# Gathering the tokens of two experts at once, already transposed, in a mixture-of-experts encoder layer

## The chip, the cores and the metric

The kernel runs on one core of one Trainium2 chip. The metric is device time in microseconds (us) of one execution, the median of several runs. Engines are named as the profile names them: PE is the matrix engine (PEld its weight loads), DVE the vector engine, ACT the scalar engine, POOL and SP the two others; SP issues nearly all transfers. SBUF is the on-chip memory with 128 partitions, PSUM the small accumulation memory that PE writes.

## The reference, cut to what matters

One encoder layer on 256 tokens of width 1024, in float32. The front half is attention beside a gated recurrence, then an output projection and a residual add. The rest, which fills most of the time, is the expert layer:

```
logits = rms_norm(x, norm2_g) @ w_router + b_router        # 32 experts
top_v, top_i = top_k(logits, 4);  gates = softmax(top_v)
for each expert e, for the tokens xb that chose it:
    g = min(xb @ w_gate[e] + b_gate[e], 7)
    u = clip(xb @ w_up[e] + b_up[e], -7, 7)
    y = ((u + 1) * g * sigmoid(1.702 * g)) @ w_down[e] + b_down[e]
out = x + sum over the chosen experts of gate * y;   final rms_norm
```

The three weight matrices of an expert are 1024 x 1024 float32, 12 MB together; 32 experts make 384 MB, and each byte is used once.

## The kernel before, in words

Weights stream through a ring of 21 slots of 1 MB. SP issues one transfer per slot, in the order gate, up, down, four pieces each, expert after expert; a transfer waits until the piece 21 slots earlier has been used by PE.

A token that chose expert e has a position in that expert's list (`pos`). The first 64 positions are handled in the main loop. Where an expert has more, a branch (`overflow`, line 866) runs a second block of 64 on the same weights before the main one; in this run that happens ahead of experts 12 and 18.

Per expert, PE does this, in program order (lines 963 to 1019):

- `ffn1` twice (lines 828 to 837): gate and up. The expert's 64 tokens, transposed (`xT`, 64 columns per 128 features), are stationary; the weights stream, 512 columns at a time, for two halves of the output that share the array, on partitions 0 to 63 and 64 to 127. `act_gate` and `act_up` apply the nonlinearity on DVE and ACT.
- In odd experts, `pair_weights` (line 883): four transposes that turn the one-hot combine weights of two experts into `gT`.
- `gather` (line 808) for the next expert: a one-hot matrix `sl` of 64 columns, scaled by the token's norm factor, is stationary and x streams, two token tiles by two halves, 512 columns each. ACT copies the 64 x 1024 result out of PSUM.
- `h_trans` (line 850): four transposes of the hidden activations, then a copy on ACT.
- `gather_trans` (line 822): four transposes of the gathered rows, then one multiply on DVE into `xT`.
- In even experts after the first, `pair_scatter` (line 912): four matmuls of 128 x 128 x 512 that add the previous pair's outputs, weighted by the gates, to four PSUM banks (`acc`) that hold the result.
- `ffn2` (line 856): the down projection, the same shape as `ffn1`, then a copy on ACT.

Transposed slices take every second column (`column_pairs`, line 818), so that two neighbouring features sit in one partition's slice of the weights. A float32 matmul is two passes in the trace, each with a weight load of its own; a transpose is one. PSUM has two buffers (`ps`, tag pt) for gathers and transposes, used in turn.

The order on each engine is the order of the code (`manual_schedule`).

Of the kernel before, what the change touches and what calls it, by code (L numbers as in the profile page):

```python
# [10 lines left out]
F32 = mybir.dt.float32  # L11
# [4 lines left out]
OP = mybir.AluOpType  # L16
# [6 lines left out]
NT = T // 128  # L23
KC = D // 128
# [47 lines left out]
def bc(ap, shape):  # L72
    return ap.to_broadcast(shape)
# [708 lines left out]
def experts(tc, A, out, g):  # L782
    nc = tc.nc
    V, S, G, PE = nc.vector, nc.scalar, nc.gpsimd, nc.tensor
    slot, x1, pos, gates, rstd2 = g["slot"], g["x1"], g["pos"], g["gates"], g["rstd2"]
    ident, iota, emask, b3, cnti = g["ident"], g["iota"], g["emask"], g["b3"], g["cnti"]
    pcols, rsqrt, weights = g["pcols"], g["rsqrt"], g["weights"]
    with ExitStack() as ctx:
        wk = ctx.enter_context(tc.tile_pool(name="wk", bufs=1))
        ps, acc = g["psum"]["ps"], g["psum"]["acc"]  # L790
        go = wk.tile([128, 512], F32, name="go")
        Y = [wk.tile([128, 512], F32, name=f"Y{d}") for d in range(2)]
# [6 lines left out]
        def pick(dst, e, b, weight):  # L799
            for t in range(NT):  # L800
                V.tensor_scalar(dst[:, t], iota[:, b], pos[:, t, e:e + 1], weight[:, t], op0=OP.is_equal, op1=OP.mult)  # L801

        def select(e, b):
            sr = wk.tile([128, NT, 64], F32, name="sro" if b else "sr")
            pick(sr, e, b, rstd2)
            return sr

        def gather(sl):
            p = ps([128, 512])
            for t in range(NT):  # L810
                for h in range(2):
                    PE.matmul(p[h * 64:h * 64 + 64, :], lhsT=sl[:, t, :], rhs=x1[:, t, h * 512:(h + 1) * 512],  # L812
                              start=t == 0, stop=t == NT - 1)
            xr = wk.tile([128, 512], F32, name="sg", tag="sg")
            S.activation(xr, p, AF.Copy)  # L815
            return xr

        def column_pairs(a, c):

            return a[:, c // 2 * 256 + c % 2:(c // 2 + 1) * 256:2]  # L820

        def gather_trans(xr, dst):
            p = ps([128, 4, 2, 64])
            for c in range(4):
                PE.transpose(p[:, c].rearrange("p a b -> p (a b)"), column_pairs(xr, c), ident)  # L825
            V.tensor_tensor(dst.rearrange("p (h c) s -> p c h s", h=2), p, n2, OP.mult)  # L826

        def ffn1(w, xT, e, which, tag="pu"):
            p = ps([128, 512], tag, 1)
            for h in range(2):  # L830
                PE.matmul(p[h * 64:h * 64 + 64, :], lhsT=bc(emask[:, e:e + 1], [96, 64]),  # L831
                          rhs=b3[:, which, h * 512:(h + 1) * 512], start=True, stop=False)
            for k in range(KC):
                for h in range(2):
                    PE.matmul(p[h * 64:h * 64 + 64, :], lhsT=xT[:, k, :],  # L835
                              rhs=w[k // 2][:, k % 2, h * 512:(h + 1) * 512], start=False, stop=k == KC - 1)
            return p

        def act_gate(p, gp):
            sg = wk.tile([128, 512], F32, name="sg", tag="sg")  # L840
            V.tensor_scalar(gp, p, LIMIT, None, op0=OP.min)  # L841
            S.activation(sg, gp, AF.Sigmoid, scale=ALPHA)  # L842
            V.tensor_tensor(gp, gp, sg, OP.mult)  # L843

        def act_up(p, gp):
            u = wk.tile([128, 512], F32, name="sg", tag="sg")
            V.tensor_scalar(u, p, LIMIT, -LIMIT, op0=OP.min, op1=OP.max)  # L847
            V.scalar_tensor_tensor(gp, u, 1.0, gp, op0=OP.add, op1=OP.mult)  # L848
# [17 lines left out]
        def overflow(cnt, e, w, b=1):  # L866

            with tc.If(cnt > 64 * b, preferred_fallthrough_block=True, label=f"ov{e}_{b}"):  # L868
                if b < 3:
                    hint(cnt, e, b + 1)  # L870
                ov_block(e, b, *w)
                if b < 3:
                    overflow(cnt, e, w, b + 1)

        def combine(e):

            gd = wk.tile([128, NT, 2, 2, 64], F32, name="gd", tag="gd")
            for u in range(2):
                for d in range(2):
                    pick(gd[:, :, d, u ^ d, :], e - 1 + u, 0, gates[:, :, e - 1 + u:e + u])  # L880
            return gd
# [25 lines left out]
        def gate_norm():  # L907
            V.tensor_reduce(gs, gates, axis=AX.X, op=OP.add)
            V.reciprocal(gs, gs)
            V.tensor_tensor(gates, gates, bc(gs, [128, NT, E]), OP.mult)  # L910

        def pair_scatter(gT, last):
            for t in range(NT):
                for d in range(2):
                    PE.matmul(acc[t][d], lhsT=gT[:, t, d, :], rhs=Y[d], start=False, stop=last)  # L915


        def one_pick(e, b, tag):
            gdo = wk.tile([128, NT, 2, 64], F32, name=tag, tag=tag)
            for u in range(2):  # L920
                pick(gdo[:, :, u], e, b, gates[:, :, e:e + 1])
            return gdo

        def one_weights(gT, gdo):
            p = ps([128, NT, 128])
            for t in range(NT):
                PE.transpose(p[:, t, :], gdo[:, t].rearrange("p a b -> p (a b)"), ident)  # L927
            S.activation(gT, p, AF.Copy)
# [7 lines left out]
        def load_cnt(e):  # L936
            c = nc.values_load(cnti[:, e:e + 1], engines=(ET.PE, ET.DVE, ET.Activation), min_val=0, max_val=T)
            hint(c, e, 1)
            return c
# [12 lines left out]
            S.activation(go, ffn2(wd, go, 0), AF.Copy)  # L952
            one_scatter(gTo, go, False)

        sl = select(0, 0)
        xT = wk.tile([128, KC, 64], F32, name="xT")
        xr = gather(sl)
        g["open_acc"](1, 1)
        gather_trans(xr, xT)
        gate_norm()  # L960
        S.activation(ssf[:, 0, 0:1], gs[:, 0], AF.Sigmoid)
        cnt = load_cnt(0)
        for e in range(E):
            last = e == E - 1
            wg, wu, wd = weights(0, e), weights(1, e), weights(2, e)
            overflow(cnt, e, (wg, wu, wd))
            gp = wk.tile([128, 512], F32, name="gp")
            if e >= E - 2:
                gd = one_pick(e, 0, "gd")
            elif e % 2 == 1:  # L970
                gd = combine(e)
            if not last:
                sl = select(e + 1, 0)
            pg = ffn1(wg, xT, e, 0, "pg")
            if not last:
                cnt = load_cnt(e + 1)
            act_gate(pg, gp)
            if last:
                one_scatter(g0, Y[0], False, (0,))
                one_scatter(g0, Y[0], False, (1,), (0,))  # L980
                g1 = wk.tile([128, NT, 2, 128], F32, name="gT", tag="gT")[:, :, 0]
                one_weights(g1, gd)
            act_up(ffn1(wu, xT, e, 1), gp)
            if e == E - 2:
                g1 = wk.tile([128, NT, 128], F32, name="g1")
                one_weights(g1, gd)
            elif e % 2 == 1 and not last:
                gT = pair_weights(gd)
            if not last:
                xr = gather(sl)  # L990
            hT = wk.tile([128, 512], F32, name="gd", tag="gd")
            h_trans(gp, hT)
            if last:
                one_scatter(g0, Y[0], False, (1,), (1,))
            else:
                xT = wk.tile([128, KC, 64], F32, name="xT")
                gather_trans(xr, xT)
            if e % 2 == 0 and e > 0:
                pair_scatter(gT, False)
            if e == 2:  # L1000
                add_b_down()
            if e < E - 2:
                py = ffn2(wd, hT, e % 2)
                for q in range(2):
                    S.activation(Y[q ^ (e % 2)][q * 64:q * 64 + 64, :], py[q * 64:q * 64 + 64, :], AF.Copy)  # L1005
            else:
                S.activation(Y[e % 2], ffn2(wd, hT, 0), AF.Copy)  # L1007
            if e == E - 2:
                g0 = g1
                fgs = slot([128, NT, D])  # L1010
                fgb, fgrow = fgs[:, 0], fgs[0:KC, 1, 0:128]
                nc.gpsimd.dma_start(fgrow, A["final_g"].rearrange("(n p) -> n p", p=128))
                for h in range(2):
                    p = ps([128, 4, 128])
                    for c in range(4):
                        k = h * 4 + c
                        PE.matmul(p[:, c, :], lhsT=bc(ident[0:KC, k:k + 1], [KC, 128]), rhs=fgrow,
                                  start=True, stop=True)
                    V.tensor_copy(fgb[:, h * 512:(h + 1) * 512], p.rearrange("p a b -> p (a b)"))
# [46 lines left out]
```

## Time and profile before

| | |
|---|---|
| time, median of 3 runs | 1096.49 us (1096.1 to 1096.49) |
| the profiled execution's own time | 1097.01 us |
| its span, first to last instruction | 1095.2 us |
| PE busy | 1046.3 us, 96% |
| DVE busy | 246.4 us, 22% |
| ACT busy | 187.2 us, 17% |
| weights and other transfers on SP's queue | 417.22 MB |

PE's matmuls are pipelined: a group's busy time covers its last pass to the modelled end, so the cost of a group within a stream is read from the start of its first instruction to the start of the next group. The transfers' rate is read from the views by stretch: 420 GB/s is what they reach when nothing holds them up.

### The profile page before, as it was taken

How to read it: one execution, taken by the hardware profiler on the slowest of the kernel's cores; microseconds unless marked ns; L12 is line 12 of the kernel's file. 1: busy time of each engine (PE TensorE's matmuls, PEld its weight loads, DVE VectorE, ACT ScalarE, POOL GpSimd, SP SyncE). 2: the span in 40 equal slices, each digit the busy share in tenths (PEclk: the TensorE clock that was granted, in tenths of full speed). 3: DMA queues.
4: the chain of work that ended last, by engine and by line, in shares of the span. 5: the costliest groups of instructions: out<-in, count | busy, mean ns of one | idle time of the engine just before them, and what ended most of it. 6: DMA issues, size and time to landing. Idle time of an engine off the chain costs nothing. (4 is left out here: it accounts for less than half of the span.)

```text
span 1095.2 us, 12179 instructions
## 1 busy us (share of the span) xinstructions
PE 1046.3 (96%) x4802; PEld 439.8 (40%) x4802; DVE 246.4 (22%) x606; ACT 187.2 (17%) x343; POOL 16.5 (2%) x29
## 2 busy tenths in 40 slices
PE   9998799999999999989999998899999999999995
PEld 7865433333333333323343332233333333333331
DVE  5674312121212121211211121121212111112111
ACT  3746401011111111110011110011111111110112
POOL 1001100000000000000000000000000000000000
PEclk9999899999999999999999999899999999999998
DMA  9954579999999999999999999499999999999993
GB/s 323 406 193 155 235 303 413 421 420 420 419 420 421 419 420 420 420 421 390 413 421 420 420 420 422 169 401 422 419 420 420 420 420 420 419 420 419 421 421 138
DMA packets 65117, 419.10 MB, mean 383 GB/s; under 512 B 6664, under 2 KB 13968, under 8 KB 15984
## 3 DMA queue, kind: packets, MB, share of 16 engines
q1 hardware_dynamic: 64832, 417.22, 92.9%
q8 instruction: 72, 1.18, 0.4%
q0 software_dynamic: 176, 0.40, 0.1%
q14 instruction: 37, 0.30, 0.1%
HBM read 416.54 MB, written 1.05 MB: 381 GB/s over the span
## 5 line engine op out<-in xcount | busy, mean ns | idle before, releaser
L862 PE MATMUL pu<-w,gd 128*64 128x512 f32 x1024 | 228.9, 600 | 0.0
L835 PE MATMUL pu<-w,xT 128*64 128x512 f32 x1024 | 226.5, 593 | 1.7 <-DMA w<-in_w_up_dram 1.6
L835 PE MATMUL pg<-w,xT 128*64 128x512 f32 x1024 | 227.5, 596 | 0.0
L835 PEld LDWEIGHTS pu<-w,xT 128*64 128x64 f32 x1024 | 83.2, 137 | 133.0 <-issue 122.2
L835 PEld LDWEIGHTS pg<-w,xT 128*64 128x64 f32 x1024 | 84.3, 138 | 121.7 <-issue 115.0
L862 PEld LDWEIGHTS pu<-w,gd 128*64 128x64 f32 x1024 | 71.2, 138 | 144.3 <-issue 137.5
L841 DVE TENSOR_SCALAR gp<-pg 128x512 f32<-128x512 f32 x32 | 22.1, 692 | 297.5 <-PE pg L835 297.5
L1005 ACT ACTIVATE Y<-pu 64x512 f32<-64x512 f32 x60 | 35.5, 592 | 273.5 <-PE pu L862 273.1
L801 DVE TENSOR_SCALAR gd<-iota,pos,gates 128x64 f32<-128x64 f32 x128 | 30.1, 309 | 155.2 <-PEq L868 155.0
L812 PE MATMUL pt<-x,sr 128*64 128x512 f32 x256 | 61.5, 599 | 0.0
L842 ACT ACTIVATE sg<-gp 128x512 f32<-128x512 f32 x32 | 20.2, 630 | 240.9 <-DVE gp L841 240.9
L847 DVE TENSOR_SCALAR sg<-pu 128x512 f32<-128x512 f32 x34 | 23.5, 692 | 163.5 <-PE pu L835 163.3
L915 PE MATMUL ps<-Y,gT 128*128 128x512 f32 x120 | 54.0, 593 | 0.0
L815 ACT ACTIVATE sg<-pt 128x512 f32<-128x512 f32 x34 | 20.3, 598 | 140.5 <-PE pt L812 140.5
L826 DVE TENSOR_TENSOR xT<-pt,prm 128x512 f32<-128x512 f32 x32 | 22.1, 692 | 70.7 <-PE pt L825 70.7
L570 PE MATMUL ps<-w 128*128 128x512 f32 x64 | 28.8, 599 | 3.5 <-DVE w L518 2.5
L915 PEld LDWEIGHTS ps<-Y,gT 128*128 128x128 f32 x120 | 21.8, 192 | 21.5 <-issue 21.5
L812 PEld LDWEIGHTS pt<-x,sr 128*64 128x64 f32 x256 | 18.0, 136 | 29.2 <-issue 24.6
L296 PE MATMUL ps<-w 128*128 128x256 f32 x128 | 28.9, 386 | 0.0
L853 PEld LDWEIGHTS pt<-ident,gp 128*128 128x128 f32 x128 | 17.8, 208 | 27.6 <-DVE gp L848 14.6
L825 PE MATMUL pt<-ident,sg 128*128 128x128 f32 x136 | 25.2, 308 | 3.6 <-ACT sg L815 1.5
L843 DVE TENSOR_TENSOR gp<-gp,sg 128x512 f32<-128x512 f32 x32 | 22.2, 693 | 24.2 <-ACT sg L842 24.2
(255 smaller groups left out, 618.5 us busy)
## 6 DMA issues: line engine op xcount, KB each, us to landing
w<-in_w_gate_dram SPq DMA_DIRECT2D x128, 1024.0 KB, 19.8
w<-in_w_up_dram SPq DMA_DIRECT2D x128, 1024.0 KB, 19.8
w<-in_w_down_dram SPq DMA_DIRECT2D x127, 1024.0 KB, 19.8
w<-in_w_in_dram SPq DMA_DIRECT2D x6, 1024.0 KB, 11.6
w<-in_w_out_dram SPq DMA_DIRECT2D x4, 1024.0 KB, 11.9
x<-in_x_dram SPq DMA_DIRECT2D x2, 512.0 KB, 4.4
w<-in_w_in_dram SPq DMA_DIRECT2D x2, 512.0 KB, 7.1
w<-in_w_down_dram SPq DMA_DIRECT2D x2, 512.0 KB, 18.3
```

The source lines that it names most:

```text
L296: PE.matmul(p, lhsT=wi[i][:, k, cs], rhs=xT[:, k, :], start=k == 0, stop=k == KC - 1)
L570: PE.matmul(p, lhsT=mT[:, kk, t * 128:(t + 1) * 128], rhs=wo[kk // 2][:, kk % 2, d * 512:(d + 1) * 512], start=k == 0, stop=k == 3)
L801: V.tensor_scalar(dst[:, t], iota[:, b], pos[:, t, e:e + 1], weight[:, t], op0=OP.is_equal, op1=OP.mult)
L812: PE.matmul(p[h * 64:h * 64 + 64, :], lhsT=sl[:, t, :], rhs=x1[:, t, h * 512:(h + 1) * 512], start=t == 0, stop=t == NT - 1)
L825: PE.transpose(p[:, c].rearrange("p a b -> p (a b)"), column_pairs(xr, c), ident)
L826: V.tensor_tensor(dst.rearrange("p (h c) s -> p c h s", h=2), p, n2, OP.mult)
L835: PE.matmul(p[h * 64:h * 64 + 64, :], lhsT=xT[:, k, :], rhs=w[k // 2][:, k % 2, h * 512:(h + 1) * 512], start=False, stop=k == KC - 1)
L843: V.tensor_tensor(gp, gp, sg, OP.mult)
L847: V.tensor_scalar(u, p, LIMIT, -LIMIT, op0=OP.min, op1=OP.max)
L862: PE.matmul(p[q * 64:q * 64 + 64, :], lhsT=hT[:, c * 128 + hf * 64:c * 128 + hf * 64 + 64], rhs=w[j // 2][:, j % 2, d * 512:(d + 1) * 512] ...
L915: PE.matmul(acc[t][d], lhsT=gT[:, t, d, :], rhs=Y[d], start=False, stop=last)
L1005: S.activation(Y[q ^ (e % 2)][q * 64:q * 64 + 64, :], py[q * 64:q * 64 + 64, :], AF.Copy)
```

## The change

The gather is done for two experts at once, and its result comes out transposed. The one-hot columns of two experts stand side by side in a tile of 128 columns (`select_pair`). A slice of x, 128 tokens by 128 features with every second column, is stationary, and the 128 one-hot columns stream. The PSUM result is x transposed for both experts, so `gather_trans`, ACT's copy and the transposes fall away in the main loop. One half of the features (`h`) is four slices by two token tiles: eight matmuls into one PSUM buffer, then one DVE multiply. The overflow block keeps the old `gather` and `gather_trans`.

Both halves are done in odd experts, one ahead of `h_trans`, one behind it. In even experts no gather is done; `pair_scatter` is cut in two, one token tile ahead of `h_trans`, the other behind it.

```diff
+        def select_pair(e):
+            sr = wk.tile([128, NT, 128], F32, name="sr")
+            for u in range(2):
+                pick(sr[:, :, u * 64:u * 64 + 64], e + u, 0, rstd2)
+            return sr
+
+        def gather_pair(sl, dst, h):
+
+            p = ps([128, 4, 128])
+            for c in range(4):
+                for t in range(NT):
+                    PE.matmul(p[:, c, :], lhsT=column_pairs(x1[:, t, h * 512:(h + 1) * 512], c), rhs=sl[:, t, :],
+                              start=t == 0, stop=t == NT - 1)
+            V.tensor_tensor(dst[:, 4 * h:4 * h + 4], p, bc(pcols("norm2_p", 4, 4 * h)[:, :, None], [128, 4, 128]), OP.mult)
...
-        def pair_scatter(gT, last):
-            for t in range(NT):
-                for d in range(2):
-                    PE.matmul(acc[t][d], lhsT=gT[:, t, d, :], rhs=Y[d], start=False, stop=last)
+        def pair_scatter(gT, t):
+            for d in range(2):
+                PE.matmul(acc[t][d], lhsT=gT[:, t, d, :], rhs=Y[d], start=False, stop=False)
...
-        sl = select(0, 0)
-        xT = wk.tile([128, KC, 64], F32, name="xT")
-        xr = gather(sl)
+        sl = select_pair(0)
+        xT = wk.tile([128, KC, 128], F32, name="xT")
+        gather_pair(sl, xT, 0)
+        gather_pair(sl, xT, 1)
         g["open_acc"](1, 1)
-        gather_trans(xr, xT)
...
-            if not last:
-                sl = select(e + 1, 0)
-            pg = ffn1(wg, xT, e, 0, "pg")
+            if e % 2 == 1 and not last:
+                sl = select_pair(e + 1)
+            xe = xT[:, :, e % 2 * 64:e % 2 * 64 + 64]
+            pg = ffn1(wg, xe, e, 0, "pg")
...
-            act_up(ffn1(wu, xT, e, 1), gp)
+            act_up(ffn1(wu, xe, e, 1), gp)
...
-            if not last:
-                xr = gather(sl)
+            if e % 2 == 1 and not last:
+                xT = wk.tile([128, KC, 128], F32, name="xT")
+                gather_pair(sl, xT, 0)
+            elif e % 2 == 0 and e > 0:
+                pair_scatter(gT, 0)
             hT = wk.tile([128, 512], F32, name="gd", tag="gd")
             h_trans(gp, hT)
...
-            else:
-                xT = wk.tile([128, KC, 64], F32, name="xT")
-                gather_trans(xr, xT)
-            if e % 2 == 0 and e > 0:
-                pair_scatter(gT, False)
+            elif e % 2 == 1:
+                gather_pair(sl, xT, 1)
+            elif e > 0:
+                pair_scatter(gT, 1)
```

PE in an odd expert before, from the up projection (`pu<-w,xT`) to the down projection (`pu<-w,gd`); x_68 is the token tile `x1`, the last number is how many alike follow each other:

```order
344 L835 MATMUL pu<-w,xT 64x512 x16
345 L887 MATMUL pt<-ident,gd 128x128 x4
346 L812 MATMUL pt<-x_68,sr 64x512 x4
347 L853 MATMUL pt<-ident,gp 128x128 x4
348 L825 MATMUL pt<-ident,sg 128x128 x4
349 L862 MATMUL pu<-w,gd 64x512 x16
```

The same place with the change:

```order
339 L850 MATMUL pu<-w,xT 64x512 x16
340 L902 MATMUL pt<-ident,gd 128x128 x4
341 L819 MATMUL pt<-sr,x_68 128x128 x8
342 L868 MATMUL pt<-ident,gp 128x128 x4
343 L819 MATMUL pt<-sr,x_68 128x128 x8
344 L877 MATMUL pu<-w,gd 64x512 x16
```

Four matmuls of 512 columns ahead of the hidden transposes and four transposes behind them have become eight matmuls of 128 columns on either side.

PE in an even expert before, over the same stretch:

```order
419 L835 MATMUL pu<-w,xT 64x512 x16
420 L812 MATMUL pt<-x_68,sr 64x512 x4
421 L853 MATMUL pt<-ident,gp 128x128 x4
422 L825 MATMUL pt<-ident,sg 128x128 x4
423 L915 MATMUL ps<-Y_996,gT 128x512
424 L915 MATMUL ps<-Y_997,gT 128x512
425 L915 MATMUL ps<-Y_996,gT 128x512
426 L915 MATMUL ps<-Y_997,gT 128x512
427 L862 MATMUL pu<-w,gd 64x512 x16
```

And with the change:

```order
414 L850 MATMUL pu<-w,xT 64x512 x16
415 L929 MATMUL ps<-Y_996,gT 128x512
416 L929 MATMUL ps<-Y_997,gT 128x512
417 L868 MATMUL pt<-ident,gp 128x128 x4
418 L929 MATMUL ps<-Y_996,gT 128x512
419 L929 MATMUL ps<-Y_997,gT 128x512
420 L877 MATMUL pu<-w,gd 64x512 x16
```

The gather and its transposes are gone from the even expert, and two of the four combine matmuls stand where the gather stood.

## Rows read from the trace of the kernel before

**Rows 1.** The page: span, busy PE, transfer rate in 40 equal slices.

```profile
span 1095.2 us, 12179 instructions
PE 1046.3 (96%) x4802; PEld 439.8 (40%) x4802; DVE 246.4 (22%) x606; ACT 187.2 (17%) x343; POOL 16.5 (2%) x29
GB/s 323 406 193 155 235 303 413 421 420 420 419 420 421 419 420 420 420 421 390 413 421 420 420 420 422 169 401 422 419 420 420 420 420 420 419 420 419 421 421 138
```

**Rows 2.** By stretch: length, busy per engine, then PE clock, DMA share, GB/s.

```profile
490.00:535.00 45.00, 43.11 (x184) 14.92 (x186) 5.78 (x15) 3.99 (x7) 0.00 (x0) 0.95 0.97 398
...
685.00:704.00 19.00, 16.53 (x64) 5.48 (x66) 0.96 (x3) 1.19 (x2) 0.00 (x0) 0.82 0.23 86
704.00:735.00 31.00, 30.77 (x140) 11.19 (x138) 5.78 (x15) 3.01 (x5) 0.00 (x0) 1.00 0.98 386
735.00:1030.00 295.00, 292.43 (x1348) 112.88 (x1346) 54.28 (x122) 36.70 (x61) 0.53 (x1) 1.00 1.01 420
```

**Rows 3.** Timeline of SP's issues at the second overflow: start, us, what.

```profile
671.21 34.94 SPq L173 DMA_DIRECT2D w<-in_w_down_dram  x4
```

**Rows 4.** Timeline of PE in expert 30, idle time before in brackets.

```profile
1032.25 1.94 PE L835 MATMUL pu<-w,xT 128*64 128x512 f32 x8 [0.55 <-DMA w<-in_w_up_dram]
...
1037.21 1.94 PE L835 MATMUL pu<-w,xT 128*64 128x512 f32 x8 [0.54 <-DMA w<-in_w_up_dram]
...
1053.26 2.05 PE L1017 MATMUL pt<-w,ident 8*128 8x128 f32 x16
```

**Rows 5.** Timeline of an even expert, from the end of up to down.

```profile
320.11 1.91 PE L812 MATMUL pt<-x,sr 128*64 128x512 f32 x8
...
321.07 0.69 DVE L848 SCALAR_TENSOR_TENSOR gp<-sg,gp 128x512 f32<-128x512 f32 x1
...
321.95 0.75 PE L853 MATMUL pt<-ident,gp 128*128 128x128 f32 x4
...
322.76 0.74 PE L825 MATMUL pt<-ident,sg 128*128 128x128 f32 x4
...
323.34 3.60 PE L915 MATMUL ps<-Y,gT 128*128 128x512 f32 x8
...
326.87 7.09 PE L862 MATMUL pu<-w,gd 128*64 128x512 f32 x32
```

**Rows 6.** Timeline of an odd expert, from the end of up to down.

```profile
348.41 0.66 PE L887 MATMUL pt<-ident,gd 128*128 128x128 f32 x4
...
349.00 1.94 PE L812 MATMUL pt<-x,sr 128*64 128x512 f32 x8
...
350.87 0.74 PE L853 MATMUL pt<-ident,gp 128*128 128x128 f32 x4
351.03 0.60 ACT L815 ACTIVATE sg<-pt 128x512 f32<-128x512 f32 x1 [1.33 <-PE pt L812]
...
351.68 0.74 PE L825 MATMUL pt<-ident,sg 128*128 128x128 f32 x4
352.36 7.09 PE L862 MATMUL pu<-w,gd 128*64 128x512 f32 x32
```

**Rows 7.** Groups by line and shape: busy us, mean ns of one, idle before.

```profile
L633 PEld LDWEIGHTS ps<-ones,w 128*128 128x128 f32 x16 | 1.9, 192 | 0.5 <-issue 0.5
L853 PEld LDWEIGHTS pt<-ident,gp 128*128 128x128 f32 x128 | 17.8, 208 | 27.6 <-DVE gp L848 14.6 <-issue 13.0
L887 PEld LDWEIGHTS pt<-ident,gd 128*128 128x128 f32 x60 | 6.3, 141 | 12.2 <-issue 12.2
L826 DVE TENSOR_TENSOR xT<-pt,prm 128x512 f32<-128x512 f32 x32 | 22.1, 692 | 70.7 <-PE pt L825 70.7
L887 PE MATMUL pt<-ident,gd 128*128 128x128 f32 x60 | 9.8, 287 | 0.0
```

**Rows 8.** Timeline about the loop's start: first gather, expert 0's first matmul.

```profile
131.00 1.94 PE L812 MATMUL pt<-x,sr 128*64 128x512 f32 x8
...
138.94 0.41 PE L831 MATMUL pg<-b,emask 96*64 96x512 bf16 x2 [4.49 <-PEq L868]
```

More of the change, by code (lines that the diff above doesn't have):

```diff
@@ L803, in select @@
         def select(e, b):
-            sr = wk.tile([128, NT, 64], F32, name="sro" if b else "sr")
+            sr = wk.tile([128, NT, 64], F32, name="sro")
             pick(sr, e, b, rstd2)
             return sr
+        def select_pair(e):
[10 more added lines that the diff above has]
+            V.tensor_tensor(dst[:, 4 * h:4 * h + 4], p, bc(pcols("norm2_p", 4, 4 * h)[:, :, None], [128, 4, 128]), OP.mult)
         def gather(sl):
```

## Prediction

> **What bounds the kernel now.** I read the page's engine rows first, then the transfer rate by slice, the views by stretch, SP's own timeline, and last PE's timeline over single experts. The page shows PE busy for 96% of the span [rows 1], which looks like a kernel bound by PE alone. The rate by slice says otherwise: from 190 us on the transfers run at 420 GB/s, with dips where an overflow block keeps PE on weights it already has [rows 1]. At 420 GB/s the 12 MB of one expert (12.58 million bytes) take 30.0 us. PE needs less: from the down projection of an even expert to that of the odd one behind it it takes 352.36 - 326.87 = 25.5 us [rows 5, 6], and an even expert 2.8 us more, since 6.76 instead of 3.95 us lie between its up and down projections. So PE eats into the ring's lead, about 3 us per expert, until an overflow fills the ring again. At the second overflow SP sits 34.94 us over four issues [rows 3], and from 685 to 704 us only 86 GB/s flow [rows 2]. From 735 us on the rate is 420 GB/s [rows 2], and in expert 30 PE has used up the lead: it waits for the pieces of the up matrix, three times 0.55 us [rows 4]. The end is thus set by both: PE's pace up to the second overflow says when the ring frees up there, the transfers' rate from there to expert 30, and PE's own chain behind that. A gain on PE between the second overflow and expert 30 only turns into waiting.
>
> What the transfers could get back at most is their loss in the stretches: 45 x (1 - 398/420) = 2.4 us, 19 x (1 - 86/420) = 15.1 us and 31 x (1 - 386/420) = 2.5 us [rows 2], 20 us in all.
>
> **The change part by part.**
>
> *Even experts.* Gather (320.11 to 321.95, with the wait for the activation inside it), four hidden transposes with a short wait (to 322.76), four gather transposes (0.58) and four combine matmuls (323.34 to 326.87, 3.53) make 6.76 us [rows 5]. Now half of the combine, 1.77 us, stands where the gather stood. The hidden transposes still wait for DVE until 1.84 us after the end of up (320.11 to 321.95) [rows 5], so this cover is as good as the old one. Then 0.58 us of transposes, and 1.77 us that hide ACT's copy of the hidden activations. 1.84 + 0.58 + 1.77 = 4.19 us: an even expert gains 2.57 us.
>
> *Odd experts.* Before: 352.36 - 348.41 = 3.95 us [rows 6]. Now: four weight transposes, 0.59 us [rows 6]; eight matmuls, that is 16 passes of 128 columns with a load of 128 columns each; the hidden transposes; 16 more passes. The trace has no pass with such a stationary operand, so the cost p of a pass is bounded by its nearest rows. With contiguous weights a float32 load of 128 columns comes every (1.9 - 0.19)/15 = 0.114 us where nothing else limits it [rows 7], and 16 passes of 128 columns with their loads take 2.05 us, (2.05 - 0.29)/15 = 0.117 us apart [rows 4, 7]. The slices of x have every second column. Rows with that step exist for transposes only: a load there is 208 ns long, against 141 ns for contiguous ones, and four of them come every (17.8/32 - 0.208)/3 = 0.116 us [rows 7]. I take 0.117 us: loads at one element per 0.116 us/128 would keep up with the rate that float32 passes have anyway. From below 0.114; from above the load may lengthen by the same 67 ns, 0.181 us, by the same ratio, 0.114 x 208/141 = 0.168 us, or cost a second load, 0.228 us.
>
> A new wait comes in. The second half needs the PSUM buffer of the first, since the hidden transposes took the other. From the first half's last pass: 0.29 us to its end [rows 7], 0.09 us until the next engine starts (350.94 to 351.03 [rows 6]), 0.69 us for DVE's multiply [rows 7], 0.19 us until PE goes on (321.76 to 321.95 [rows 5]), some 0.1 us for the first load behind a wait. The hidden transposes cover 0.58 us of it. The stretch is 0.59 + 15p + 0.29 + 0.09 + 0.69 + 0.19 + 0.1 + 16p = 1.95 + 31p = 5.58 us: an odd expert loses 1.63 us. Behind the waiting matmuls stands the down projection; its hidden activations are ready by then.
>
> [...]
>
> *What goes or comes beside PE.* ACT loses a copy per expert, DVE has the same two picks and one multiply per expert; both engines are 17% and 22% busy and cover it. In expert 0 nothing stands between up and the hidden transposes; their wait takes the place of the gather, within 0.3 us. Ahead of the loop 16 plus 16 passes (3.7 us) replace 1.9 us of gather and a copy, transposes and a multiply; expert 0 starts 7.9 us after the gather began, most of it PE's sequencer (4.49 us [rows 8]), so I count zero there, with 2 us to either side.
>
> *The sum.* Up to the second overflow lie 8 even experts that gain (2 to 16) and 9 odd ones that lose (1 to 17): 8 x 2.57 - 9 x 1.63 = 5.9 us. The ring frees up by that much earlier. Behind it expert 18's down pieces free another 2.57 us earlier, which returns about half of that stretch's 2.5 us loss, 1.3 us (bounds 0 and 2.5). From 735 us on the rate decides, and the further 0.94 us per pair on PE become waits, up to expert 30's up matrix. Behind that point expert 30 gains its 2.57 us once more, if the last pieces arrive in time (bounds 0 and 2.57). 5.9 + 1.3 + 2.57 = 9.8 us off the profiled execution's 1097.01 us gives 1087.2; it is 0.5 us above the median of the runs, so 1086.7 us. PE alone would gain 15 x 0.94 = 14.1 us; the transfers keep 4 of these.
>
> **Rivals.**
>
> *The loads of every second column pace the passes: slower.* In each odd expert the gather then takes 1.95 + 31p. It decides from p = 0.151 us on, where the loss per pair, 2.68 us, is the gain plus the 1.6 us of waits in expert 30 spread over 15 pairs. PE then sets the whole time: with 0.168 us 15 x (3.21 - 2.57) - 1.6 = 8 us slower, 1104.5; with 0.181 us 14 us, 1110.5; with 0.228 us 36 us, 1132. For it: the 67 ns in [rows 7]. Against: the spacing of these loads, 0.116 us, is no more than an ordinary float32 load takes. [...]
>
> *The transfers hide it.* If the ring does not free up earlier at the second overflow, only expert 30's 2.57 us remain: 1094 us. For it: 420 GB/s in nearly every slice [rows 1]. Against: SP's 34.94 us there end when PE takes up expert 18's weights [rows 3].
>
> *The new wait is not paid,* because the second half's start overlaps it: odd experts lose 0.8 us, 8 x 2.57 - 9 x 0.8 + 1.3 + 2.57 = 17 us, 1079.5 us. Against: two buffers used in turn.
>
> **How the numbers follow.** Forecast 0.70, slow loads 0.19, hidden 0.06, no wait 0.05. The forecast's own range is 1083 to 1091: p from 0.114 to 0.127 moves the sum by 0.8 us up and 2.8 us down, the start by 2 us. For 8 in 10 I reach to 1081 and to 1106, which takes in the hidden case, the mildest of the slow loads and a part of the no-wait case. A difference under 0.2% (2.2 us) is about what a measurement cannot tell from none. Faster: the forecast, no wait, and about half of hidden, 0.77; same: the rest of hidden and p near 0.15, 0.05; slower 0.18.
>
> **What would show it.** In the changed trace: the passes of L819 0.117 us apart; 4.2 us between up and down in even experts, 5.6 in odd ones; a wait for DVE ahead of the second half; a shorter dip after the second overflow, which begins and ends 6 us earlier; and more and earlier waits of PE for weights ahead of expert 30. Passes over 0.15 us apart, or a dip that ends no earlier, would prove me wrong.

## The result: 1% faster, and the profile after

The changed kernel takes 1082.73 us (median of 4 runs, 1081.23 to 1089.44), the kernel before 1096.3 us beside it (4 runs, 1092.68 to 1096.49). The ratio is 0.9896, 95% interval 0.9848 to 0.9943. The forecast was 1086.7 us with a range of 1081 to 1106; the result lies just below the forecast's own 1083 to 1091. The profiled execution took 1084.03 us, 13.0 us less than the profiled 1097.01 of before; the steps below are compared against that difference.

The page of the changed kernel, span and transfer rate in 40 slices, answers to [rows 1]:

```profile
span 1082.3 us, 12372 instructions
...
GB/s 325 406 201 141 253 303 413 420 420 420 420 420 421 420 420 419 420 422 420 420 421 418 420 421 421 256 422 420 420 420 421 419 420 420 420 421 420 420 420 166
```

The dip at slices 19 and 20 (390 and 413 before) is gone, and the one at slice 26 is shallower. The view by stretch of the changed kernel (length, busy time per engine, granted PE clock, DMA share, GB/s) answers to [rows 2]:

```profile
490.00:535.00 45.00, 43.62 (x200) 15.48 (x198) 6.92 (x18) 3.64 (x6) 0.00 (x0) 1.00 1.01 420
680.00:698.00 18.00, 16.78 (x74) 5.15 (x72) 0.00 (x0) 0.60 (x1) 0.00 (x0) 0.91 0.49 180
698.00:735.00 37.00, 36.52 (x179) 15.50 (x176) 9.00 (x21) 4.24 (x7) 0.00 (x0) 1.00 1.01 419
735.00:960.00 225.00, 222.30 (x1082) 94.08 (x1082) 39.44 (x89) 22.86 (x38) 0.00 (x0) 1.00 1.01 420
```

Measured against 420 GB/s, the transfers lost 2.4, 15.1 and 2.5 us in the three stretches of before, 20.0 in all. Now they lose nothing in the first, 18 x (1 - 180/420) = 10.3 us in the second and 37 x (1 - 419/420) = 0.1 us in the third: 9.6 us less. The stall that makes the dip is in SP's timeline of the changed kernel at the second overflow (start, us, what), 27.21 us over four issues where [rows 3] has 34.94:

```profile
669.57 27.21 SPq L173 DMA_DIRECT2D w<-in_w_down_dram  x4
```

PE's timeline of an even expert in the changed kernel, from the end of up to down, answers to [rows 5]:

```profile
317.61 1.98 PE L929 MATMUL ps<-Y,gT 128*128 128x512 f32 x4
...
319.43 0.63 PE L868 MATMUL pt<-ident,gp 128*128 128x128 f32 x4
319.89 1.88 PE L929 MATMUL ps<-Y,gT 128*128 128x512 f32 x4
321.70 7.09 PE L877 MATMUL pu<-w,gd 128*64 128x512 f32 x32
```

321.70 - 317.61 = 4.09 us lie between up and down (4.19 expected, 6.76 before). PE and DVE in the odd expert behind it (idle time and what ended it in brackets) answer to [rows 6]:

```profile
343.24 0.66 PE L902 MATMUL pt<-ident,gd 128*128 128x128 f32 x4
343.74 2.05 PE L819 MATMUL pt<-sr,x 128*128 128x128 f32 x16
...
345.62 0.63 PE L868 MATMUL pt<-ident,gp 128*128 128x128 f32 x4
345.82 0.69 DVE L821 TENSOR_TENSOR xT<-pt,prm 128x512 f32<-128x512 f32 x1 [1.05 <-PE pt L819]
...
346.57 2.15 PE L819 MATMUL pt<-sr,x 128*128 128x128 f32 x16 [0.32 <-DVE xT L821]
...
348.65 7.09 PE L877 MATMUL pu<-w,gd 128*64 128x512 f32 x32
```

5.41 us (5.58 expected, 3.95 before). Sixteen passes take 2.05 us, so (2.05 - 0.29)/15 = 0.1175 us apart; and the second half waits for DVE's multiply on the first, 0.32 us that the hidden transposes leave open. From the first gate matmul of one expert to that of the next, an even expert fell from 28.17 to 25.64 us and an odd one rose from 25.485 to 26.95: -2.53 and +1.47, so 1.07 us a pair. No run has the pair gather with the combine left whole, so what cutting `pair_scatter` in two adds by itself was not measured.

The groups of the changed kernel by line and shape (busy us, mean ns of one, idle time before and what ended it):

```profile
L819 PE MATMUL pt<-sr,x 128*128 128x128 f32 x512 | 68.0, 287 | 4.7 <-DVE xT L821 4.7
L819 PEld LDWEIGHTS pt<-sr,x 128*128 128x128 f32 x512 | 63.9, 199 | 8.7 <-DVE xT L821 7.6 <-issue 1.1
...
L850 PE MATMUL pu<-w,xT 128*64 128x512 f32 x1024 | 227.8, 593 | 4.6 <-DMA w<-in_w_up_dram 4.5
L850 PE MATMUL pg<-w,xT 128*64 128x512 f32 x1024 | 226.3, 592 | 0.9 <-DMA w<-in_w_gate_dram 0.9
```

The wait for DVE adds up to 4.7 us in the whole kernel. The last two rows say where part of the gain was lost: PE waits 4.6 + 0.9 = 5.5 us for weights by the brackets; before it was three waits of about 0.55 us, all in expert 30 [rows 4]. They begin in expert 28, two experts earlier, as PE's timeline of the changed kernel shows:

```profile
967.07 1.94 PE L850 MATMUL pu<-w,xT 128*64 128x512 f32 x8 [0.54 <-DMA w<-in_w_up_dram]
...
1028.64 0.44 PE L941 MATMUL pt<-ident,gd 128*128 128x128 f32 x2
...
1032.91 7.25 PE L877 MATMUL pu<-w,gd 128*64 128x512 f32 x32
```

PE's timeline of the kernel before has, at the same place:

```profile
1039.08 0.44 PE L927 MATMUL pt<-ident,gd 128*128 128x128 f32 x2
...
1046.24 7.09 PE L862 MATMUL pu<-w,gd 128*64 128x512 f32 x32
```

Expert 30's up ends at 1028.64 us, 10.4 us earlier than before (1039.08), and 1032.91 - 1028.64 = 4.27 us lie between its up and down against 7.16 before: 2.9 us more. Together 13.3, of which 13.0 reach the profiled time.

### The profile page after: what moved, and what is told of

It reads as the page before. It is cut to its first block, busy times and chain, and to the rows that moved or that the text cites. A ratio compares the mean times of both kernels' runs of the same rounds, so it can differ in the third digit from the quotient of the medians.

```text
span 1082.3 us, 12372 instructions
## 1 busy us (share of the span) xinstructions
PE 1027.9 (95%) x4930; PEld 463.3 (43%) x4930; DVE 244.8 (23%) x606; ACT 168.2 (16%) x311; POOL 16.8 (2%) x29
## 5 line engine op out<-in xcount | busy, mean ns | idle before, releaser
L819 PE MATMUL pt<-sr,x 128*128 128x128 f32 x512 | 68.0, 287 | 4.7 <-DVE xT L821 4.7
L819 PEld LDWEIGHTS pt<-sr,x 128*128 128x128 f32 x512 | 63.9, 199 | 8.7 <-DVE xT L821 7.6
L929 PE MATMUL ps<-Y,gT 128*128 128x512 f32 x120 | 57.9, 605 | 0.0
L869 ACT ACTIVATE gd<-pt 128x512 f32<-128x512 f32 x32 | 19.1, 597 | 159.0 <-PE pt L868 159.0
L846 PEld LDWEIGHTS <-emask 96*64 96x64 bf16 x136 | 9.1, 107 | 43.7 <-issue 39.7
L296 PEld LDWEIGHTS ps<-w 128*128 128x128 f32 x128 | 24.1, 190 | 4.1 <-DVE w L280 0.6
```

The costliest lines, as they stand in the source:

```text
L296: PE.matmul(p, lhsT=wi[i][:, k, cs], rhs=xT[:, k, :], start=k == 0, stop=k == KC - 1)
L819: PE.matmul(p[:, c, :], lhsT=column_pairs(x1[:, t, h * 512:(h + 1) * 512], c), rhs=sl[:, t, :], start=t == 0, stop=t == NT - 1)
```

## The experiments

Nine kernels ran, in three groups that shared runs of the kernel before. In the expectations theory A is the account of the prediction: PE's work up to the second overflow moves the time, work behind it turns into waits for weights or out of them, and the passes are paced by their float32 loads. What stands against it is named in each.

### The same extra work behind and ahead of the second overflow

`late_work` runs the four weight transposes of odd experts three times, in experts 19 to 29:

```
-        def pair_weights(gd):
+        def pair_weights(gd, times=1):
...
-            for t in range(NT):
+            for t in [t for _ in range(times) for t in range(NT)]:
...
-                gT = pair_weights(gd)
+                gT = pair_weights(gd, 3 if e > 18 else 1)
```

> The changed kernel with the four weight transposes of each odd expert from 19 to 29 done three times over: 6 x 8 extra transposes, about 0.87 us per odd expert, 5.2 us of added PE work, all of it behind the second overflow. Theory A (behind the second overflow the transfers set the pace up to expert 30, PE waits there anyway): the waits for weights, 5.5 us in the changed kernel's experts 28 to 30, shrink by what is added; time 0 to 1 us longer. Theory B (PE's work sets the time throughout): 5.2 us longer.

`early_work` has the same edit with `e < 18`, so in experts 1 to 17.

> The same extra transposes in the odd experts 1 to 17: 9 x 0.87 = 7.8 us of added PE work ahead of the second overflow. Theory A: the ring frees up 7.8 us later at the second overflow, the dip there is that much longer, and the time grows by 7 to 8 us, 1:1, while the same work behind the overflow is nearly free. Theory B: 7.8 us longer too. A third theory (the transfers hide all of PE's work): no change in either run.

Late work: 1085.04 us (1081.98 to 1087.85, 6 runs), ratio to the kernel before 0.9899, interval 0.9869 to 0.9928, the changed kernel's 0.9896 within the noise. Its profiled span is 1082.4 us against 1082.3, though six experts carry 0.87 us more each, 5.2 us in all (in expert 29 the transposes take 1.36 us instead of 0.50, so 0.86). Expert 31 starts at 1043.60 us, against 1043.21. The work went into waits that shrank. In the group view of late_work, up's waits for weights are 2.4 us instead of 4.6, and gate's 0.9 us are gone:

```profile
L850 PE MATMUL pu<-w,xT 128*64 128x512 f32 x1024 | 226.7, 592 | 2.4 <-DMA w<-in_w_up_dram 2.4
```

These are 3.1 us less, and the brackets show only a part of the waits: from expert 28's gate to expert 31's it takes 85.26 us instead of 89.25, with 0.87 us more work in it, so 4.9 us of waiting less.

Early work: 1089.87 us (1085.14 to 1093.01, 9 runs), ratio 0.9938, interval 0.9914 to 0.9961, so 4.8 us over late work beside it, less than the 7 to 8 expected; over the changed kernel's medians (1082.73, and 1081.88 in a later group) it is 7.1 and 8.0. From expert 3's first gate matmul to expert 18's it takes 473.48 us instead of 467.07: 6.4 us more, where 8 x 0.87 = 7.0 were put in. Behind that nothing is made up: from expert 18 to expert 31 early work takes 352.30 us and the changed kernel 352.13. The stall at the overflow is longer again, as SP's timeline of early_work shows:

```profile
669.07 30.32 SPq L173 DMA_DIRECT2D w<-in_w_down_dram  x4
```

Three microseconds more than the 27.21 of the changed kernel; late_work has 25.94. Theory A holds in its main point: extra work on PE lengthens the way to expert 18 nearly one to one and stays lost, and behind the second overflow, where the ring was last full, it turns into waits that shrink.

### The wait for DVE between the two halves

`second_bank` puts the second half of the gather into a PSUM buffer that gate uses elsewhere, so that it does not wait for the multiply on the first half:

```
-            p = ps([128, 4, 128])
+            p = ps([128, 4, 128], "pg", 1) if h else ps([128, 4, 128])
```

> The changed kernel, with the second half of the pair gather written to the PSUM bank of the gate projection, which is free by then, so that it need not wait for DVE to empty the first half. The wait goes from some 0.45 us per odd expert (start of the hidden transposes to start of the second half, 0.95 us, less 0.5 of transposes) to nothing. Theory A: 9 x 0.45 = 4 us earlier at the second overflow, 3 to 4 us faster than the changed kernel; behind the overflow the gain becomes waits for weights. Theory B (PE alone): 15 x 0.45 = 6.8 us faster. If the wait was no cost, because the loads are what stands there: no change.

1079.86 us (1076.43 to 1084.98, 6 runs), ratio 0.9857, interval 0.9824 to 0.989. PE's timeline of an odd expert in second_bank has no bracket behind its second half any more:

```profile
340.82 0.63 PE L868 MATMUL pt<-ident,gp 128*128 128x128 f32 x4
341.29 2.05 PE L819 MATMUL pg<-sr,x 128*128 128x128 f32 x16
343.27 7.09 PE L877 MATMUL pu<-w,gd 128*64 128x512 f32 x32
```

The stretch fell from 5.41 to 4.83 us. The 0.58 us are more than the 0.32 us of the bracket: in the changed kernel the second half starts 0.95 us after the hidden transposes (345.62 to 346.57), here 0.47 us after them (340.82 to 341.29), and its passes take 2.15 us there and 2.05 here.

The time of the whole kernel shows less. The changed kernel's medians are 1082.73 and 1081.88 us, so second_bank is 2 to 3 us faster, where the expectation had 3 to 4, and that is not clear of the scatter. The profiled spans differ by 5.5 us (1082.3 and 1076.8), but that is mostly luck: 3.6 of it lie ahead of expert 3, where the edit should give 0.6 (it starts at 220.37 us instead of 224.01), and from expert 3 to 18 second_bank gains only 1.1 us (465.98 against 467.07), where eight odd experts should give 4.6. PE now runs out of weights already in expert 11, ahead of the first overflow, where the changed kernel does not wait. PE's timeline of second_bank there:

```profile
436.48 1.94 PE L850 MATMUL pu<-w,xT 128*64 128x512 f32 x8 [0.33 <-DMA w<-in_w_up_dram]
438.97 1.94 PE L850 MATMUL pu<-w,xT 128*64 128x512 f32 x8 [0.56 <-DMA w<-in_w_up_dram]
```

From expert 11's gate to expert 12's it takes 66.12 us instead of 62.72. In the whole kernel the waits for weights rose as well, in the group view of second_bank:

```profile
L850 PE MATMUL pu<-w,xT 128*64 128x512 f32 x1024 | 228.6, 594 | 7.9 <-DMA w<-in_w_up_dram 7.9
```

### What the step of two columns costs

`plain_slices` takes neighbouring columns of x instead of every second one:

```
-PE.matmul(p[:, c, :], lhsT=column_pairs(x1[:, t, h * 512:(h + 1) * 512], c), rhs=sl[:, t, :],
+PE.matmul(p[:, c, :], lhsT=x1[:, t, h * 512 + c * 128:h * 512 + (c + 1) * 128], rhs=sl[:, t, :],
```

> The changed kernel with contiguous slices of x in place of every second column; the features reach the wrong rows of the weights, so the computed values differ. If the step of two columns costs nothing beyond the usual float32 load: passes of the gather stay 0.115 to 0.117 us apart, loads 192 instead of 199 ns, time unchanged within 1 us. If the step sets the spacing: passes come closer, 0.107 us or less, the 16 passes take 1.8 instead of 2.05 us, and the dip at the second overflow begins 4 us earlier.

One run, 1078.27 us; one run is too few for the time, but the groups are clear. In plain_slices they read:

```profile
L819 PE MATMUL pt<-sr,x 128*128 128x128 f32 x512 | 63.8, 278 | 4.8 <-DVE xT L821 4.6
L819 PEld LDWEIGHTS pt<-sr,x 128*128 128x128 f32 x512 | 59.5, 192 | 8.4 <-DVE xT L821 7.5 <-issue 0.9
```

A load takes 192 ns instead of 199, and 16 passes 1.95 us instead of 2.05, so (1.95 - 0.28)/15 = 0.1115 us apart instead of 0.1175. The step costs 6 ns a pass, 0.19 us per odd expert: little, and not nothing, and between the two cases of the expectation. A load that is 7 ns shorter brought the passes 6 ns closer, so the load paces them.

### Two experts at a time, or one

`one_expert` keeps the transposed form and gathers for one expert at a time; 64 columns stream per pass, there are twice as many passes, and the combine stands whole behind the gather again:

```
-            sr = wk.tile([128, NT, 128], F32, name="sr")
-            for u in range(2):
-                pick(sr[:, :, u * 64:u * 64 + 64], e + u, 0, rstd2)
+            sr = wk.tile([128, NT, 64], F32, name="sr")
+            pick(sr, e, 0, rstd2)
...
-            elif e % 2 == 1:
+            else:
                 gather_pair(sl, xT, 1)
-            elif e > 0:
+            if e % 2 == 0 and e > 0:
+                pair_scatter(gT, 0)
                 pair_scatter(gT, 1)
```

> The transposed form for one expert at a time: the same slices of x stationary, 64 one-hot columns stream, 32 passes in every expert in place of 32 per pair. Theory A (the 128-column weight load sets the spacing of the passes, whatever streams): passes stay 0.11 to 0.12 us apart, PE takes some 2.5 to 3 us more per pair than the kernel before, and the time is 35 to 45 us longer than before. Rival (the streaming columns set the spacing): passes 0.055 to 0.07 us apart, PE's work as in the pair form or less, time 1080 to 1090 us.

1134.51 us (1130.26 to 1135.64, 4 runs), ratio 1.037, interval 1.034 to 1.0401: 39.4 us slower than before, as theory A had it: 2.6 us a pair (29.67 + 26.57 us against 28.17 + 25.485), and no wait for weights. PE's timeline of one_expert shows two of its groups of 16 passes (lines are one lower in this kernel):

```profile
352.26 1.99 PE L818 MATMUL pt<-sr,x 128*128 128x64 f32 x16
...
378.33 2.10 PE L818 MATMUL pt<-sr,x 128*128 128x64 f32 x16
```

Half the columns, the same time: 1.99 to 2.10 us for 16 passes, against 2.05 with 128 columns. With plain_slices, where a load of 192 instead of 199 ns brought the passes from 0.1175 to 0.1115 us apart, this shows that these passes are paced by their weight loads, and the second expert's 64 columns ride along for nothing. That is where the gain of the pair form comes from.

### With the transfers out of the way

`before_short` and `after_short` are the two kernels with a shorter weight stream:

```
-    plan = [("o", 0, c) for c in (0, 1, 2, 3)] + [(m, e, c) for e in range(E) for m in range(3) for c in range(4)]
+    plan = [("o", 0, c) for c in (0, 1, 2, 3)] + [(m, e, c) for e in range(E) for m in (0, 2) for c in range(4)]
...
-            wg, wu, wd = weights(0, e), weights(1, e), weights(2, e)
+            wg, wd = weights(0, e), weights(2, e)
+            wu = wg
```

> The kernel before with the up weights left out of the stream: up is computed with the gate's weights, so 8 MB per expert are loaded in place of 12, and the values differ. The transfers then need 20 us per expert, less than PE, and cannot hold it up. Without the waits for weights in expert 30 (1.6 us), 1094 to 1097 us.

> The changed kernel with the same shorter stream. Theory A (the full stream keeps part of the gain): the difference to the kernel before with the short stream is all of PE's gain, 15 x 1.07 = 16 us and up to 2 us from the start, 16 to 18 us, against 13 us with the full stream. Theory B (PE's work alone sets the time in both): the same 13 us as with the full stream. No wait for weights is left in the expert loop.

before_short takes 1094.9 us (10 runs), ratio to the kernel before 1.0006, interval 0.9987 to 1.0024; after_short 1074.53 us (4 runs), ratio 0.9813, interval 0.9782 to 0.9845. From 735 us on the rate is down to 314 GB/s in before_short,

```profile
735.00:1000.00 265.00, 262.74 (x1208) 101.27 (x1206) 47.66 (x109) 32.46 (x54) 0.53 (x1) 1.00 0.81 314
```

and to 317 in after_short,

```profile
735.00:1000.00 265.00, 261.83 (x1273) 111.31 (x1274) 49.14 (x111) 27.11 (x45) 0.53 (x1) 1.00 0.82 317
```

and neither kernel waits for weights in the loop. The kernel before does not gain from a third fewer bytes: PE alone sets its time, but for the waits in expert 30. With PE alone the change is worth 17.5 us between the profiled executions (1093.73 and 1076.27) and 20.4 between the medians; with the whole stream it was 13.0 and 13.6. So the transfers keep 4.5 to 6.8 us. The experts say the same: 28 to 30 take 89.25 us in the changed kernel and 81.28 in after_short, 8.0 us of waiting, and expert 30 takes 33.98 in the kernel before and 31.39 in before_short, 2.6 us; the difference is 5.4. The brackets, 5.5 and 1.6 us, show only a part of these waits.

### The changed kernel again, and a version that beats both

`after_again` is the changed kernel without an edit, run beside `best_order`.

> The changed kernel itself once more, beside the runs that are compared with it. 1081 to 1085 us; by the profiled executions so far single runs scatter by some 4 us with the number of half-clock stretches of TensorE, so the trace's own places (start of expert 18, last weight landed) are what is compared.

1081.88 us (1080.68 to 1084.46, 4 runs), ratio 0.9892, interval 0.9859 to 0.9925. Expert 3 to 18 takes 466.59 us, against 467.07 in the first profile and 473.45 before (473.08 in before_short).

`best_order` adds to second_bank another order in the overflow block, so that DVE and ACT work on the hidden activations while PE is still in up:

```
-            pg, pu = ffn1(wg, xo, e, 0, "pg"), ffn1(wu, xo, e, 1)
-            one_weights(gTo, one_pick(e, b, "sro"))
+            pg = ffn1(wg, xo, e, 0, "pg")
             act_gate(pg, go)
-            act_up(pu, go)
+            gdo = one_pick(e, b, "sro")
+            act_up(ffn1(wu, xo, e, 1), go)
+            one_weights(gTo, gdo)
             h_trans(go, go)
```

> The changed kernel with the second half in the gate's PSUM bank, and the overflow block in another order: there ACT's sigmoid of the gate stands behind ACT's copy of the combine weights, which waits for the end of the up projection; now the gate's activation comes first, and the combine weights' transposes stand behind up. PE's idle time ahead of the hidden transposes in each overflow block, 3.34 us, becomes some 1.4 us. [...]

1079.23 us (1078.35 to 1080.05, 4 runs), ratio 0.9861, interval 0.9832 to 0.9891. It is faster than both kernels (its slowest run is below the fastest of after_again); from second_bank, 1079.86 us, it can't be told apart. I had 1074 to 1076 us for it: two times 1.9 us less idle time, all of it paid, and by an estimate up to 2.5 us a block if the down projection takes 7.09 instead of 9.58 us. That was missed; the rival, that the stall at the second overflow is not what PE frees, had 1080 us, no change against second_bank. PE's timeline of the changed kernel in the second overflow block has

```profile
676.27 1.10 PE L868 MATMUL pt<-ident,go 128*128 128x128 f32 x4 [3.34 <-DVEq L883]
678.06 9.58 PE L877 MATMUL pu<-w,go 128*64 128x512 f32 x32 [0.69 <-ACT go L869]
```

and best_order has

```profile
668.24 0.72 PE L868 MATMUL pt<-ident,go 128*128 128x128 f32 x4 [1.24 <-DVEq L883]
669.65 7.09 PE L877 MATMUL pu<-w,go 128*64 128x512 f32 x32 [0.69 <-ACT go L869]
```

The edit did there what it was to do: 2.1 us less idle, and the down projection takes 7.09 instead of 9.58 us. At the first overflow the idle time is the same, but the down projection is not short:

```profile
479.23 0.72 PE L868 MATMUL pt<-ident,go 128*128 128x128 f32 x4 [1.24 <-DVEq L883]
480.64 8.78 PE L877 MATMUL pu<-w,go 128*64 128x512 f32 x32 [0.69 <-ACT go L869]
```

Expert 18 starts at 680.18 us, 6.2 earlier than in second_bank, and SP's stall is down to 16.17 us:

```profile
669.70 16.17 SPq L173 DMA_DIRECT2D w<-in_w_down_dram  x4
```

The time did not follow. The groups of best_order by line say why:

```profile
L850 PE MATMUL pg<-w,xT 128*64 128x512 f32 x1024 | 231.2, 600 | 4.4 <-DMA w<-in_w_gate_dram 4.4
...
L850 PE MATMUL pu<-w,xT 128*64 128x512 f32 x1024 | 229.3, 594 | 9.9 <-DMA w<-in_w_up_dram 9.9
```

14.3 us of waits for weights, against 9.9 in second_bank; in both the first are already in expert 11, at 433 and 434 us. The dip is almost gone: the transfers of best_order run at 420 GB/s from 490 to 535 us, 421 from 660 to 680, 403 from 680 to 715 and 420 from 735 to 960; the last weights landed at 1061.2 us, only 1.1 earlier than in second_bank (1062.3), though PE was 6.2 us ahead at expert 18. So here most of the work taken off PE became waiting. A longer ring wasn't tried.

## Why the prediction was right, point by point

**The bound.** Both parts held: the kernel before is set by PE but for 2.6 us in expert 30 (before_short), and with the change the rate decides behind the second overflow (late_work against early_work). PE alone was to gain 14.1 us, of which the transfers were to keep 4; it gains 17.5 (profiled) to 20.4 (medians), and they keep 4.5 to 6.8.

**The even expert's gain,** 2.57 us, measured 2.53 from expert to expert. The halves of the combine cover what the gather covered.

**The odd expert's loss,** 1.63 us, measured 1.47. The pass was taken at 0.117 us and is 0.1175. The other 1.95 us of the stretch came out at 5.41 - 31 x 0.1175 = 1.77: from the end of the first half (343.74 + 2.05 = 345.79) to the start of the second (346.57) it is 0.78 us, where I had 0.09 + 0.69 + 0.19 + 0.1 = 1.07. The multiply starts 0.03 us behind the first half instead of 0.09 (345.82), takes 0.69, and PE goes on 0.06 us behind it instead of 0.19. The 0.1 us for the first load does appear, inside the second half (2.15 us instead of 2.05). The four weight transposes take 0.50 us, where I had 0.59.

**What the loads cost.** Against the 67 ns that [rows 7] show between the loads of two kinds of transposes, the step of two columns costs these loads 7 ns: 199 against 192 ns in plain_slices, and 6 ns a pass. The three lengthened passes, 0.168, 0.181 and 0.228 us, were estimates, and no run shows them. A load takes 199 ns where the passes stand 0.1175 us apart, so it runs beside earlier passes; and in one_expert, with 64 columns streaming, the passes are (1.99 - 0.283)/15 = 0.114 to (2.10 - 0.283)/15 = 0.121 us apart, no closer than with 128.

**The total,** 9.8 us predicted, 13.0 between the profiled executions. Up to expert 18 I had 5.9 us and no gain at the start. With the measured sizes it is 8 x 2.53 - 9 x 1.47 = 7.0. Expert 18 starts 9.4 us earlier, by PE's timeline of the kernel before

```profile
700.46 7.03 PE L835 MATMUL pg<-w,xT 128*64 128x512 f32 x32
```

and of the changed kernel:

```profile
691.08 7.04 PE L850 MATMUL pg<-w,xT 128*64 128x512 f32 x32
```

From there to the end of expert 30's up I had 1.3, and it is 10.4 - 9.4 = 1.0. Expert 30 gave 2.9 instead of 2.57. These make 7.0 + 1.0 + 2.9 = 10.9. Two terms were mis-sized: the odd expert's loss, 9 x 0.16 = 1.4 us up to expert 18, and the start, taken as 0 with 2 us either way: expert 0's gate ends 1.8 us earlier. Of the 13.0 some 0.3 remains that I can't place.

Whether the start belongs to the change stays open. Its pieces differ from run to run of the same kernel. The start of the changed kernel's loop, PE's timeline in the first profile, which answers to [rows 8]:

```profile
131.25 4.97 PE L819 MATMUL pt<-sr,x 128*128 128x128 f32 x32
...
138.88 0.41 PE L846 MATMUL pg<-b,emask 96*64 96x512 bf16 x2 [1.80 <-PEq L883]
139.09 7.06 PE L850 MATMUL pg<-w,xT 128*64 128x512 f32 x32
```

and the same in after_again, the same kernel:

```profile
129.77 4.01 PE L819 MATMUL pt<-sr,x 128*128 128x128 f32 x32
...
136.81 0.41 PE L846 MATMUL pg<-b,emask 96*64 96x512 bf16 x2 [2.17 <-PEq L883]
137.03 8.76 PE L850 MATMUL pg<-w,xT 128*64 128x512 f32 x32
```

The gather takes 4.97 us in the one and 4.01 in the other, gate 7.06 and 8.76, and yet gate ends near 146 us in both. Over the profiles of the changed kernel and its variants gate ends between 143.7 and 148.4 us, mean 146.1 of eight (one_expert left out); over those of the kernel before and before_short at 147.9 and 147.5. The gain of some 1.6 us is smaller than that scatter. What can't be luck is the stretch from expert 3 to 18, 467.07 and 466.59 against 473.45.

**The rivals.** Slow loads fell with 0.1175 us (0.151 was the point from which they decide). Hidden by the transfers fell with the stall, which ends 9.4 us earlier. That the wait is not paid fell with the bracket of 0.32 us in every odd expert, and second_bank shows what it would have been worth: 0.58 us an expert. The time alone would not have told: 1082.73 us lies 4.0 us below the forecast and 3.2 above that rival's 1079.5.

## What to carry to other kernels

Here 16 float32 passes took 1.99 to 2.10 us with 64 columns streaming and 2.05 with 128, each pass paced by its weight load; ask what else could stream past the same weights, since doubling 64 columns to 128 cost no time, and one expert at a time took 52 us longer than two. Where a ring of transfers and an engine share the bound, find the last place where the ring is full: here 7.8 us of work put in ahead of it cost 7.1 to 8.0 us over the changed kernel's medians, and of 5.2 us put in behind it 4.9 went into waits that shrank. Work taken off ahead of it can turn into waiting too: second_bank and best_order ran out of weights in expert 11, ahead of the first overflow, and by the brackets waited 9.9 and 14.3 us in all, where the changed kernel waited 5.5. Then work out how much is left until the stream has no gaps, here about 10 us of dip in the changed kernel, as a bound on what work taken off the engine can still give ahead of it.

## What the hardware showed that I had not expected

Runs of one kernel scatter by several us, in step with the mean granted clock: the four runs of the changed kernel took 1081.23 us at 0.985, 1081.43 at 0.984, 1084.03 at 0.981 and 1089.44 at 0.978. In the traces these are stretches in which the same 32 matmuls take 8.75 to 9.84 us instead of 7.1, at a granted clock of 0.50 instead of 1.00 for a part. The view by stretch of expert 0's gate, in the kernel before:

```profile
139.00:144.00 5.00, 5.00 (x18) 1.92 (x20) 0.00 (x0) 0.00 (x0) 0.00 (x0) 0.66 0.17 34
```

and in the changed kernel:

```profile
139.00:144.00 5.00, 5.00 (x26) 2.04 (x26) 0.00 (x0) 0.00 (x0) 0.00 (x0) 1.00 0.38 121
```

The 0.66 is a mean: by shorter stretches the kernel before has 1.00 from 139.0 to 139.5 us, 0.50 from 140.0 to 143.0 and 1.00 from 143.5 to 144.0, and the changed kernel 1.00 in each of them. PE had been idle 4.49 us before the one [rows 8] and 1.80 before the other; in after_again it was 2.17 us, and gate took 8.76. But one_expert's gate took 7.06 us behind 2.27 us of idle time, so the length of the wait does not separate them. Nor does it in the overflow blocks: behind the same 1.24 us of idle time best_order's down projection took 7.09 us at the second overflow and 8.78 at the first; behind 3.34 us the changed kernel's took 9.58 and 9.05. That a wait on PE costs more than its length, by a lower clock in the work behind it, is therefore not shown. How the clock falls in one run and not in another at the same place, these runs do not tell.
